# A hybrid decoder layer on one Trainium2 core: modulation sums, first loads and the whole hand-written order are rewritten

## Chip, core and metric

One core of one Trainium2 chip runs the whole layer as one program. The time is the device time of one execution in microseconds; lower is better. Engines: TensorE (PE, matrix products; its loads of the stationary operand are listed as PEld), VectorE (DVE), ScalarE (ACT), GpSimd (POOL), SyncE (SP, issues DMAs). ScalarE has a DMA queue as well, which is called the second queue here.

## The reference, cut to what matters

x is 256 x 1024, c is 1 x 1024, all in float32, one layer:

```python
mod = c @ w_ada + b_ada                                  # 1024 -> 3072
shift, scl, gate = split(mod, 3)
h = rms_norm(x, g_norm) * (1 + scl) + shift
proj = h @ w_in                                          # 1024 -> 5120
u_pool, z_pool, q, k, v, z_attn, m_pool, m_attn = split(proj)
y_pool = (multiscale_pool(u_pool) * silu(z_pool)) @ w_pool_up
y_attn = (attention(rope(q), rope(k), v) * silu(z_attn)) @ w_attn_up
merged = sigmoid(m_pool) * y_pool + sigmoid(m_attn) * y_attn
out = rms_norm(x + gate * (merged @ w_out), g_final)
```

With 256 positions and attention blocks of 256 there is one block, so the attention is plain causal attention of 8 heads of 64.

## The kernel before, in words

**Split products.** Each product with a weight runs as three products on rounded operands: a weight `raw` as loaded is rounded by ScalarE to `whi` (token `hi`, L223), VectorE forms the rest `wlo = raw - whi` (token `lo`, L227), and the activations are split the same way (hh and hl). The three are whi·hh, whi·hl and wlo·hh. So each unit of weights passes DMA, then ScalarE, then VectorE, then TensorE.

**Units.** The weights are cut into units. A0 to A7 are the rows k of w_in for q, k and v (768 KB each, one k block of 128 rows and 1536 columns). F1, F3, F5a, F5b, U, ZP, ZAa, ..., MA1b hold parts of the other columns of w_in, UP0 to UP3 the up projections, OUT0 to OUT3 w_out, G0 to G3 the part of w_ada for the gate, at most 1 MB each. A unit takes one of five `raw` buffers, and whi and wlo have three buffers each. `LOADS` is the order of the loads, all on SP's queue; `pump` (L199) is called when the last split of a unit is written and queues the next loads for which a buffer is free. Integers in `LOADS` are the parts of w_ada for shift and scale: 0, 1, 4, 5, 6 and 7 are one block of 128 outputs (1 MB), 2 covers blocks 2 and 3 (2 MB). 4 and 5 reuse the tile of 0 and 1, and 6 and 7 that of 2, so they wait for these. SP issues in order: a load that waits for its buffer holds up all behind it.

**The order.** `PROGRAM` is a list of tokens; a loop at the end of the kernel turns each into a call by the dictionary `table`, and each engine executes its own instructions in the order in which the tokens stand. Engines wait for one another by data and buffers alone. So the place of a token counts against those of the same engine.

**Start.** x is loaded in two halves of 128 rows. ScalarE squares (L412), GpSimd forms rstd, VectorE scales (xn, L418), TensorE transposes in blocks of 128 (`x`, L348), ScalarE copies the blocks from PSUM to xnT (`xc`, L351). `warm` is a transpose of the identity into a bank that is overwritten later; it gives nothing to the result (L309). The modulation of block k: either VectorE sums eight products with c over the tile (`mod_acc`, L263 and L265), or TensorE does it against c repeated in 32 columns (`mod_pe`, L291), or half each, and `mod_out` brings the sum to SBUF (L299, L302). It then stands spread over 128 partitions. `mod_fin` (L318) multiplies it by a column of ones, which sums over the partitions and gives one value per partition; `mod_add` adds the bias and multiplies the scale by the norm weight (L326, L327). Then `hh` (L358), `h` (L365) and `hl` (L368) make the split activations of block k.

**Projections.** `ap` is one of the three passes of a unit A for one of three column groups i and one of two row blocks t, 128x512 (L387); `a` is all three. The six results stay in six PSUM banks over all k. `f` is a job of an F unit, three 128x256 products for each of its k blocks (L372 to L374). `evac` brings q, k and v to SBUF, `rope` rotates, `tr` and `trc` transpose, `sc` are the scores; softmax, attention and the pooling follow.

**End.** `up` forms the up projections, `mg` to `mgl` the gated merge, `out:f:n` adds the part of feature block f to output bank n (banks 0 and 1: rows 0 to 127; 2, 3 and 4: rows 128 to 255, of 512, 256 and 256 columns). The gate is a row: `gate:0` to `gate:7` sum on VectorE, `gatef` (L668) sums over partitions, `gatec` copies it, writes it to DRAM and reads it back to all partitions as gg (L676, L677). `res` multiplies a bank by gg (L741), `resx` adds x, `sq` squares, `rstd` runs on GpSimd, `weigh`, `sact` and `sdve` scale, `store` writes out.

Of the kernel before, what the change touches and what calls it, by code (L numbers as in the profile page):

```python
# [78 lines left out]
ap:0:2:1:2 ap:1:1:0:0 ap:0:0:0:2 ap:1:0:0:0 hl:1 ap:1:0:0:1 hi:F1:0:512 ap:1:0:1:0 lo:F1:0:512 ap:1:1:1:1 f:F1:0
f:F1:1 ap:1:1:1:0 hi:F1:512:1024 lo:F1:512:1024 hi:A1:1024:1536 ap:1:2:1:0 f:F1:2 mod_acc:2:0:4 f:F1:3 hi:F1:1024:1536  # L80
lo:F1:1024:1536 ap:1:1:0:1 lo:A1:1024:1536 mod_pe:2:4:8 hi:F1:1536:2048 mod_out:2 ap:1:2:1:1 ap:1:2:0:2 ap:1:2:0:0
ap:0:1:1:1 fin:F1:0 fin:F1:1 hi:A2:512:1024 hi:A2:0:512 hi:A2:1024:1536 lo:A1:512:1024 mod_fin:2:0 mod_fin:2:1
mod_add:2:0 h:2 hh:2 ap:1:1:0:2 ap:1:2:0:1 f:F1:4 f:F1:5 mod_add:2:1 ap:1:0:1:1 ap:2:2:1:0 ap:2:1:0:0 h:3 ap:1:0:0:2
# [786 lines left out]
```

## Time and profile before

| | us |
|---|---|
| median of 3 runs (lowest to highest) | 204.57 (204.27 to 205.05) |
| the profiled execution | 204.59 |
| its span, first to last instruction | 202.8 |

| engine | busy, us | share of the span | instructions |
|---|---|---|---|
| TensorE products | 191.3 | 94% | 1412 |
| TensorE loads of operands | 172.3 | 85% | 1412 |
| VectorE | 153.6 | 76% | 278 |
| ScalarE | 111.4 | 55% | 195 |
| GpSimd | 6.5 | 3% | 19 |

The DMA engines moved 46.73 MB, 230 GB/s in the mean. The mean granted clock of TensorE was 0.994 of full speed. How to read it: the page is of one execution, and times count from its first instruction. Products are pipelined, and a busy TensorE need not be at its peak; the distance between the starts of neighbouring products says more. In the chain of waits each piece is the work that the next one waited for. "[0.32 <-DVE hh]" behind a row means that the engine was idle 0.32 us before it and what ended that.

### The profile page before, as it was taken

Reading aid. Unit: us, or ns where it says so; the run is one execution under the profiler, and the core shown is the slowest. Engines: PE = TensorE matmul, PEld = TensorE weight load, DVE = VectorE, ACT = ScalarE, POOL = GpSimd, SP = SyncE. Lnnn points to the kernel's source line nnn. Section 1 sums busy time; section 2 is a strip of 40 time slices with the busy share of each in tenths; the row PEclk is TensorE's granted clock in tenths of the full one; section 3 lists DMA queues with packets and bytes.
Section 4 is the critical chain, followed back from the end, with each engine's and each line's share of the span. In section 5 each row is a group of like instructions: output and inputs, shape, how many; then the busy total and the mean of one; then the engine's idle time right before and its main releaser. Section 6 shows DMA issues by size and latency. Waiting matters only on the chain.

```text
span 202.8 us, 3615 instructions
## 1 busy us (share of the span) xinstructions
PE 191.3 (94%) x1412; PEld 172.3 (85%) x1412; DVE 153.6 (76%) x278; ACT 111.4 (55%) x195; POOL 6.5 (3%) x19
## 2 busy tenths in 40 slices
...
GB/s 158 385 424 411 414 314 253 387 419 417 346 205 239 207 158 86 224 204 7 367 259 207 124 247 160 175 194 378 414 419 74 207 210 0 140 171 5 0 103 103
DMA packets 10921, 46.73 MB, mean 230 GB/s; under 512 B 1684, under 2 KB 2584, under 8 KB 8216
## 3 DMA queue, kind: packets, MB, share of 16 engines
...
q10 hardware_dynamic: 576, 0.41, 0.7%
q8 instruction: 11, 0.18, 0.3%
...
q0 software_dynamic: 32, 0.00, 0.0%
HBM read 45.44 MB, written 1.05 MB: 229 GB/s over the span
## 4 chain that ended last, share of the span: by engine, by line
PE 77%; DMA 13%; issue 3%; DVE 2%; ACT 1%; SPq 1%; POOL 1%; POOLq 0%; DVEq 0%; ACTq 0%
PE acc L372 15%; PE acc L373 14%; PE acc L374 14%; PE acc L387 12%; DMA ada<-in_ada_one_dram 10%; PE misc L372 4%; PE misc L373 4%; PE misc L374 4%; DMA x<-in_x_dram 3%; PE misc L291 2%; PE acc L472 1%; PE acc L541 1%; PE acc L594 1%; PE misc L318 1%; SPq L196 1%
## 5 line engine op out<-in xcount | busy, mean ns | idle before, releaser
L227 DVE TENSOR_TENSOR wlo<-raw,whi 128x1024 fp32r<-128x1024 f32 (+2 forms) x70 | 68.2, 1007 | 15.3 <-ACT whi L223 14.8
L223 ACT CAST whi<-raw 128x1024 fp32r<-128x1024 f32 (+2 forms) x70 | 57.9, 876 | 26.1 <-PE acc L387 7.7
L372 PE MATMUL acc<-hh,whi 128*128 128x256 f32 x168 | 47.9, 285 | 0.0
L373 PE MATMUL acc<-hh,wlo 128*128 128x256 f32 x168 | 46.9, 279 | 0.0
L374 PE MATMUL acc<-hl,whi 128*128 128x256 f32 x168 | 46.8, 279 | 0.0
L372 PEld LDWEIGHTS acc<-hh,whi 128*128 128x128 f32 x168 | 31.6, 188 | 0.6 <-DVE stat L491 0.3
L373 PEld LDWEIGHTS acc<-hh,wlo 128*128 128x128 f32 x168 | 31.6, 188 | 0.1
L374 PEld LDWEIGHTS acc<-hl,whi 128*128 128x128 f32 x168 | 31.6, 188 | 0.0
L387 PE MATMUL acc<-whi,hh 128*128 128x512 f32 x42 | 15.6, 406 | 0.4 <-DVE hh L358 0.3
L372 PE MATMUL misc<-hh,whi 128*128 128x256 f32 x56 | 15.7, 280 | 0.0
L373 PE MATMUL misc<-hh,wlo 128*128 128x256 f32 x56 | 15.6, 279 | 0.0
L374 PE MATMUL misc<-hl,whi 128*128 128x256 f32 x56 | 15.6, 279 | 0.0
L387 PE MATMUL acc<-whi,hl 128*128 128x512 f32 x42 | 15.4, 401 | 0.0
L387 PE MATMUL acc<-wlo,hh 128*128 128x512 f32 x42 | 14.9, 404 | 0.0
L373 PE MATMUL acc<-whi,mhl 128*128 128x512 f32 (+1 forms) x40 | 13.9, 348 | 0.0
L372 PE MATMUL acc<-whi,mhl 128*128 128x512 f32 (+1 forms) x40 | 13.9, 348 | 0.0
L374 PE MATMUL acc<-wlo,mhl 128*128 128x512 f32 (+1 forms) x40 | 13.9, 346 | 0.0
L373 PEld LDWEIGHTS misc<-hh,wlo 128*128 128x128 f32 x56 | 10.5, 188 | 0.4
L372 PEld LDWEIGHTS misc<-hh,whi 128*128 128x128 f32 x56 | 10.5, 188 | 0.4
L265 DVE SCALAR_TENSOR_TENSOR adacc<-ada,vT,adacc 128x256 f32<-128x256 f32 (+1 forms) x19 | 10.0, 527 | 0.7
L374 PEld LDWEIGHTS misc<-hl,whi 128*128 128x128 f32 x56 | 10.5, 188 | 0.0
L309 PE MATMUL acc<-ident 128*128 128x128 f32 x52 | 9.1, 336 | 1.4 <-POOL ident masks.py:199 1.4
...
## 6 DMA issues: line engine op xcount, KB each, us to landing
raw<-in_weights_dram SPq DMA_DIRECT2D x19, 1024.0 KB, 4.9
...
ada<-in_ada_one_dram SPq DMA_DIRECT2D x11, 512.0 KB, 8.9
ada<-in_ada_two_dram SPq DMA_DIRECT2D x4, 512.0 KB, 11.6
g<-in_weights_dram SPq DMA_DIRECT2D x2, 1024.0 KB, 8.5
...
x<-in_x_dram SPq DMA_DIRECT2D x2, 512.0 KB, 5.9
raw<-in_x_dram SPq DMA_DIRECT2D x1, 1024.0 KB, 5.1
```

The source lines that it names most:

```text
L196: nc.sync.dma_start(t[:, i:i + step], weights[:, OFFSET[u] + i:OFFSET[u] + i + step])
L223: nc.scalar.copy(halves[u][0][:, a:b], raws[u][:, a:b])
L227: nc.vector.tensor_tensor(lo[:, a:b], raws[u][:, a:b], hi[:, a:b].bitcast(F32), op=ALU.subtract)
L265: nc.vector.scalar_tensor_tensor(a, t[:, kt], cT[:, kt:kt + 1], a, op0=ALU.mult, op1=ALU.add)
L291: nc.tensor.matmul(peb[k][r0:r0 + 32, 0:2 * n * P], c_rep[:, kt], t[:, kt].rearrange("p s n -> p (s n)"), start=kt < 4 or k in sums, stop= ...
L309: nc.tensor.transpose(banks_qkv[0][1][:, 0:P], ident, ident)
L318: nc.tensor.matmul(r[:, s:s + 1], sums[k][:, s, i * P:(i + 1) * P], ones[:, 0:1], start=True, stop=True)
L372: nc.tensor.matmul(o, ah, bh, start=start, stop=False)
L373: nc.tensor.matmul(o, al, bh, start=False, stop=False)
L374: nc.tensor.matmul(o, ah, bl, start=False, stop=stop)
L387: nc.tensor.matmul(banks_qkv[i][t], act[:, k, t * P:(t + 1) * P], halves[f"A{k}"][w][:, i * 512:(i + 1) * 512], start=k == 0 and p == 0, s ...
L472: nc.tensor.matmul(bv[j][:, i], qkT[0][r, h // 2, t * P:(t + 1) * P], qkT[0][r, 4 + h // 2, 0:nkeys], start=True, stop=True)
```

## The change

It does the following:

- The vector of small parameters (vT: c, norm weight, biases) is loaded first on the second queue, ahead of a first piece of ada 0 that is now two k blocks instead of one; the rest of ada 0 comes in pieces of four and two k blocks.
- xnT takes the norm weight already when it is copied from PSUM, block by block: blocks 0 and 1 on ScalarE, 2 to 7 on VectorE. The modulation no longer multiplies by it.
- For all blocks but 0, the sum over partitions is made by transposing the sums on TensorE (`mod_tr`) and reducing along the free axis on VectorE (`mod_red`), in place of the products with ones; one small add then gives shift and scale together.
- The loads have another order.
- All of `PROGRAM` is new.

The code, with the order cut to the places named later:

```diff
 LOADS = """
-A0 1 A1 F1 2 A2 A3 F3 A4 4 5 F5a A5 F5b 6 7 A6 consts ZP A7 MP0b U MP1b ZAa ZAb MP0a MP1a G0 G1 MA0a MA0b MA1b
-MA1a UP1 UP0 OUT0 OUT1 UP3 UP2 gf OUT2 OUT3 xr
+A0 1 A1 F1 2 A2 A3 F3 4 A4 6 F5a 5 A5 7 A6 F5b U A7 ZAb MP0b ZP consts MP1a MP0a MA0a ZAa MA1b MP1b MA0b G0 UP1 MA1a
+UP3 G1 OUT0 UP0 UP2 OUT2 xr OUT1 OUT3 gf
 """.split()
 PROGRAM = """
-warm:30 x:0:1:0 x:1:1:0 x:2:2:0 x:4:2:0 x:6:2:0 warm:3 x:0:1:1 x:1:1:1 xc:0:1 x:2:2:1 xc:1:1 x:4:2:1 xc:2:2 x:6:2:1
-warm:2 mod_pe:0:0:4 xc:4:2 warm:5 mod_pe:0:4:8 mod_out:0 warm:6 mod_fin:0:0 mod_add:0:0 hi:A0:0:512 hh:0 warm:6 h:0
+warm:32 x:0:1:0 x:1:1:0 x:2:2:0 x:4:2:0 x:6:2:0 mod_pe:0:0:2 mod_pe:0:2:6 warm:3 x:0:1:1 xc:0:1:0 mod_pe:0:6:8
+mod_out:0 x:1:1:1 x:2:2:1 x:4:2:1 x:6:2:1 xc:1:1:0 mod_fin:0:0 xc:2:2:1 mod_add:0:0 hi:A0:0:512 hh:0 h:0 warm:8 hl:0
+xc:4:2:1 xc:6:2:1 hi:A0:512:1024 ap:0:0:1:0 ap:0:0:0:0 ap:0:0:0:1 ap:0:0:1:1 hi:A0:1024:1536 lo:A0:0:512 mod_pe:1:0:8
+mod_out:1 ap:0:1:0:0 ap:0:1:0:1 ap:0:2:0:0 ap:0:2:0:1 mod_tr:1 ap:0:1:1:0 ap:0:1:1:1 lo:A0:512:1024 ap:0:0:1:2
...
+hh:7 ap:6:0:0:0 h:7 ap:7:1:1:0 hl:7 ap:6:1:0:1 ap:7:1:0:0 ap:7:2:0:1 ap:7:1:1:1 ap:7:0:0:1 ap:7:2:0:0 lo:A7:0:768
+ap:5:2:0:2 ap:6:0:0:1 ap:5:2:1:0 ap:5:1:1:1 ap:7:0:0:0 lo:A7:768:1536 ap:7:1:0:1 ap:7:1:0:2 hi:ZP:0:1024 ap:6:0:1:0
+lo:ZP:0:1024 ap:6:2:1:2 ap:6:2:1:0 ap:7:2:1:1 ap:5:0:0:2 ap:7:2:1:0 hi:ZP:1024:2048 ap:7:2:1:2 ap:7:1:1:2 evac:1:1
+evac:1:0 ap:5:0:0:0 hi:U:0:1024 ap:5:0:0:1 ap:6:2:0:2 ap:7:0:0:2 evac:0:0 ap:7:0:1:1 ap:7:0:1:0 lo:ZP:1024:2048
+ap:6:0:1:2 ap:7:0:1:2 evac:0:1 hi:ZAb:1024:1536 f:ZP:0 f:ZP:1 lo:U:0:1024 f:U:2 evac:2:1 f:U:3 f:U:0 f:U:1 rope:1
+fin:ZP:0 rope:0 tr:1 fin:F5b:0 tr:3 hi:ZAb:0:1024 hi:MP0a:0:1024 hi:MP0a:1024:1536 fin:U:1 fin:U:0 tr:0 trc:0 trc:3
...
+mg:3 mgl:5 mga:3 mgh:3 gate:7 gatef mgl:3 mg:2 out:4:4 mg:7 mga:7 mga:2 hi:OUT1:1024:2048 mgh:2 hi:OUT1:0:1024
+lo:OUT1:1024:2048 out:3:2 out:3:0 out:3:1 mgh:7 mgl:2 lo:OUT1:0:1024 out:5:1 out:2:1 out:2:4 out:3:4 out:2:2 gatec
+mg:6 mga:6 hi:OUT3:0:1024 hi:OUT3:1024:2048 lo:OUT3:0:1024 lo:OUT3:1024:2048 out:3:3 mgh:6 mgl:6 out:2:0 out:6:0
+out:5:0 out:2:3 mgl:7 out:7:0 res:0 resx:0 out:6:1 out:7:1 res:1 resx:1 sq:0:0 sq:1:0 weigh:0 out:5:2 out:6:2 weigh:1
+out:4:2 out:7:2 res:2 resx:2 out:5:3 out:6:3 out:4:3 out:7:3 res:3 resx:3 sq:2:0 out:6:4 out:5:4 out:7:4 mean:0 res:4
+resx:4 sq:3:0 mean:1 rstd:0 sact:0 store:0:0 sq:4:1 rstd:1 sact:1 store:1:0 weigh:2 sact:2 sdve:4:0 store:4:1
+store:2:0 sdve:3:0 store:3:1
 """
     xs = work.tile([P, NT, D], F32, name="x", tag="qk", bufs=1)
+    nc.scalar.dma_start(vT, vecs)
...
-        for i in range(0, NK, step):
-            a = i
-            if k == i == 0:
-                nc.scalar.dma_start(t[:, 0:1], src[:, 0:1])
-                nc.scalar.dma_start(vT, vecs)
-                a = 1
-            nc.sync.dma_start(t[:, a:i + step], src[:, a:i + step])
+        ends = (2, 6, 8) if k == 0 else range(step, NK + 1, step)
+        for i, j in zip((0, *ends), ends):
+            queue = nc.scalar if k == i == 0 else nc.sync
+            queue.dma_start(t[:, i:j], src[:, i:j])
...
+    def mod_tr(k):
+        n = 1 if k in ONES else 2
+        sum_banks[k] = misc()
+        for i in range(n):
+            for s in range(2):
+                nc.tensor.transpose(sum_banks[k][:, (2 * i + s) * P:(2 * i + s + 1) * P],
+                                    sums[k][:, s, i * P:(i + 1) * P], ident)
+        used.add(k)
+        pump()
+
+    def mod_red(k):
+        n = 1 if k in ONES else 2
+        r = work.tile([P, 4], F32, name="modr")
+        nc.vector.tensor_reduce(r[:, 0:2 * n], sum_banks[k][:, 0:2 * n * P].rearrange("p (a b) -> p a b", b=P), axis=AX.X,
+                                op=ALU.add)
+        nc.vector.tensor_tensor(mods[:, k:k + n], r[:, 0:2 * n].rearrange("p (a b) -> p a b", b=2), bias[:, k:k + n],
+                                op=ALU.add)
+
     def mod_add(k, i):
-        r, ks = sum_banks[k][:, 2 * i:2 * i + 2], slice(k + i, k + i + 1)
-        nc.vector.tensor_scalar(scale[:, ks], r[:, 1:2], bs1[:, ks], gT[:, ks], op0=ALU.add, op1=ALU.mult)
-        nc.vector.tensor_tensor(shift[:, ks], r[:, 0:1], bT[:, ks], op=ALU.add)
+        nc.vector.tensor_tensor(mods[:, k + i], sum_banks[k][:, 2 * i:2 * i + 2], bias[:, k + i], op=ALU.add)
...
-    def x_copy(k, n):
-        nc.scalar.copy(xnT[:, k:k + n].rearrange("p a b -> p (a b)"), xbanks[k][:, 0:n * S])
+    def x_copy(k, n, dve):
+        for j in range(n):
+            src, g = xbanks[k][:, j * S:(j + 1) * S], gT[:, k + j:k + j + 1]
+            if dve:
+                nc.vector.tensor_scalar(xnT[:, k + j], src, g, None, op0=ALU.mult)
+            else:
+                nc.scalar.activation(xnT[:, k + j], src, AF.Copy, scale=g)
```

`bias` holds b_ada of shift and 1 + b_ada of scale side by side, made by two small VectorE instructions at the start, and `mods` shift and scale side by side; `hh` and `h` read them from there.

## Rows read from the trace of the kernel before

**Rows 1.** The page's table of engines: busy us (share of the span) xinstructions.

```profile
PE 191.3 (94%) x1412; PEld 172.3 (85%) x1412; DVE 153.6 (76%) x278; ACT 111.4 (55%) x195; POOL 6.5 (3%) x19
```

**Rows 2.** Stretches: us, busy of PE, PEld, DVE, ACT, POOL, granted clock, DMA share, GB/s.

```profile
0.00:30.00 30.00, 26.91 (x184) 21.12 (x185) 13.97 (x32) 15.60 (x30) 3.08 (x14) 1.00 0.91 352
30.00:40.00 10.00, 10.00 (x64) 8.91 (x63) 9.45 (x19) 5.59 (x9) 0.00 (x0) 1.00 0.89 315
100.00:120.00 20.00, 20.00 (x173) 20.00 (x172) 18.07 (x36) 15.39 (x21) 0.00 (x0) 1.00 0.60 211
```

**Rows 3.** Timeline, start: begin us, us, engine, line, operation [idle before <-releaser].

```profile
7.33 0.29 DVE L245 TENSOR_SCALAR c_rep<-vT 128x256 f32<-128x256 f32 x1 [7.33 <-DMA vT<-in_vecs_dram]
...
9.31 0.92 DVE L418 TENSOR_SCALAR xn<-x,rstd 128x512 f32<-128x512 f32 x2 [0.82 <-POOL rstd L334]
...
12.36 0.64 PE L291 MATMUL misc<-ada,c_rep 128*32 128x256 f32 x8
...
13.64 0.52 PE L318 MATMUL misc<-ones,adapart 128*128 128x1 f32 x4
...
14.64 0.41 DVE L358 TENSOR_SCALAR hh<-xnT,scale,shift 128x256 fp32r<-128x256 f32 x1
...
15.20 0.71 PE L387 MATMUL acc<-whi,hh 128*128 128x512 f32 x2 [0.32 <-DVE hh L358]
```

**Rows 4.** Chain of waits in order of time: begin us, us, what.

```profile
1.20 5.93 DMA x<-in_x_dram
...
19.43 0.34 PE misc L318 x4
...
68.22 9.33 PE acc L387 x40
...
85.91 0.87 PE misc L453 x8
```

**Rows 5.** Timeline, 17 to 50 us: SP's issues, hh, and TensorE's wait.

```profile
17.64 0.33 SPq L196 DMA_DIRECT2D raw<-in_weights_dram  x1
...
28.60 1.28 SPq L196 DMA_DIRECT2D raw<-in_weights_dram  x3
...
29.53 0.41 DVE L358 TENSOR_SCALAR hh<-xnT,scale,shift 128x256 fp32r<-128x256 f32 x1
...
49.72 1.07 PE L291 MATMUL misc<-ada,c_rep 128*32 128x256 f32 x16 [1.41 <-DMA ada<-in_ada_one_dram]
```

**Rows 6.** Groups by line and form: xcount | busy us, mean ns | idle before <-releasers.

```profile
L227 DVE TENSOR_TENSOR wlo<-raw,whi 128x1024 fp32r<-128x1024 f32 x39 | 46.6, 1221 | 10.6 <-ACT whi L223 10.6
...
L326 DVE TENSOR_SCALAR scale<-misc,bs,vT 128x1 f32<-128x1 f32 x8 | 2.2, 276 | 7.8 <-ACT whi L223 4.0 <-PE misc L318 3.8
...
L489 DVE TENSOR_TENSOR pr<-acc,mask 128x256 f32<-128x256 f32 x4 | 1.7, 418 | 0.0
...
L223 ACT CAST whi<-raw 128x1024 fp32r<-128x1024 f32 x39 | 39.5, 1049 | 12.5 <-PE acc L387 5.9 <-issue 3.6 <-PE acc L374 1.1
...
L365 ACT ACTIVATE h<-xnT,shift,scale 128x256 f32<-128x256 f32 x8 | 4.6, 597 | 9.4 <-DVE shift L327 9.4
...
L351 ACT COPY xnT<-misc 128x256 f32<-128x256 f32 x1 | 0.4, 373 | 1.9 <-PE misc L348 1.9
```

**Rows 7.** DMA issues: operand, queue, xcount, KB each, median us to landing.

```profile
raw<-in_weights_dram SPq DMA_DIRECT2D x19, 1024.0 KB, 4.9
...
gg<-gdram SPq DMA_DIRECT2D x1, 512.0 KB, 3.7
```

**Rows 8.** Timeline, end: gate row and last output banks.

```profile
174.02 0.64 PE L668 MATMUL misc<-gg,ones 128*32 128x256 f32 x8
...
178.86 0.33 SPq L677 DMA_DIRECT2D gg<-gdram  x1
...
188.22 0.69 DVE L741 TENSOR_TENSOR r<-acc,gg 128x512 f32<-128x512 f32 x1 [1.69 <-PE acc L374]
...
195.85 0.42 DVE L741 TENSOR_TENSOR r<-acc,gg 128x256 f32<-128x256 f32 x1 [0.18 <-PE acc L374]
```

More of the change, by code (lines that the diff above doesn't have):

```diff
@@ L79 @@
[L79 to L83, printed above, removed]
@@ L119 @@
-hi:UP2:0:1024 lo:UP2:0:1024 hi:UP2:1024:2048 lo:UP2:1024:2048 up:0:0 gate:6 up:1:1 mg:1 fin:MA1b:0 hi:OUT0:1024:2048
-hi:OUT0:0:1024 up:0:1 mg:0 up:4:0 up:4:1 up:5:0 gate:5 up:5:1 mga:1 lo:OUT0:1024:2048 lo:OUT0:0:1024 mga:0 mgh:0
-gate:7 up:2:0 mgl:0 up:2:1 fin:MA1a:0 mg:4 mga:4 up:3:0 up:3:1 fin:MA0b:0 mgh:1 mgl:1 out:0:3 hi:UP3:1024:2048 out:0:0
-out:1:3 hi:UP3:0:1024 lo:UP3:0:1024 out:0:1 out:1:1 hi:OUT1:1024:2048 hi:OUT1:0:1024 out:0:2 out:1:2 mg:3 mga:3 mgh:3
-mgh:4 mgl:4 out:0:4 out:1:4 mgl:3 lo:OUT1:1024:2048 out:3:4 out:3:3 out:1:0 out:3:1 mg:5 mga:5 gatef lo:OUT1:0:1024
@@ L124 @@
-gatec up:7:0 lo:UP3:1024:2048 up:7:1 mgh:5 hi:OUT2:1024:2048 hi:OUT2:0:1024 out:3:2 mg:2 mga:2 up:6:0 up:6:1
-lo:OUT2:0:1024 out:4:1 out:4:0 mgh:2 mgl:2 out:2:3 mg:7 out:3:0 mga:7 out:2:1 mgh:7 out:2:0 out:2:4 mgl:7 out:2:2
-lo:OUT2:1024:2048 hi:OUT3:0:1024 lo:OUT3:0:1024 hi:OUT3:1024:2048 mgl:5 out:5:0 mg:6 mga:6 mgh:6 lo:OUT3:1024:2048
-mgl:6 out:6:0 out:7:0 out:6:1 res:0 resx:0 out:5:1 out:7:1 res:1 resx:1 sq:0:0 weigh:0 sq:1:0 out:4:2 mean:0 rstd:0
-sact:0 out:5:2 out:6:2 out:7:2 store:0:0 res:2 weigh:1 sact:1 out:6:3 store:1:0 resx:2 sq:2:0 out:4:3 out:5:3 out:7:3
@@ new lines @@
+lo:MP0b:0:1024 hi:MP0b:1024:1536 pool:0 f:ZAa:1 fin:ZAa:0 lo:MP0b:1024:1536 f:MP0a:0 f:MP0a:1 scm:1:1:2 scm:1:5:2
+fin:ZAb:0 exp:0:0:4 hi:MP1a:0:1024 hi:MP1a:1024:2048 lo:MP1a:0:1024 lo:MP1a:1024:2048 exp:1:4:2 norm:1:4:2 f:MP0b:0
+f:MP0b:1 fin:MP0a:0 f:MP1a:0 f:MP1a:1 exp:1:1:2 norm:1:1:2 att:1 exp:1:5:2 hi:MP1b:0:1024 hi:MP1b:1024:2048
+lo:MP1b:1024:2048 lo:MP1b:0:1024 f:MP1b:0 fin:MP0b:0 sco:1:0:2 silu:2560:1 hi:MA0a:0:1024 f:MP1b:1 hi:MA0a:1024:2048
+scm:1:0:2 lo:MA0a:1024:2048 lo:MA0a:0:1024 f:MA0a:0 f:MA0a:1 exp:1:0:2 norm:1:0:2 silu:512:0 silum:512:0
```

90 lines of the change are left out of this document (43 added, 47 removed).

## The prediction

> **What bounds the kernel now.** I read the busy table first: TensorE is busy for 94% of the span, VectorE for 76%, ScalarE for 55% [rows 1]. A busy share hides where the limit changes, so next came the stretches [rows 2]. From 100 to 120 us TensorE is busy for all 20 us at granted clock 1.00, its 2.4 GHz level; from 30 to 40 us it is full as well, and VectorE beside it works 9.45 of 10. Whether full means packed is read from the chain of waits in order of time [rows 4]: 40 projection passes of 128x512 in a row take 9.33 us, 0.233 each, and long pieces like this one, on TensorE alone, fill it from 15.2 to 195.8 us, where the last product ends. So the time is: a start, 180.6 us of nearly gapless TensorE work, and a tail. An edit pays only if it starts that stream earlier, takes a hole or an instruction out of it, or shortens the tail; what it moves on other engines counts only where TensorE then waits.
>
> The start is read from the timeline [rows 3]. The second half of x lands at 7.1 us [rows 4]; square, rstd and the scaled xn follow (9.31) [rows 3], then its transposes, and only after these stand in TensorE's queue the modulation products of block 0 (those of its last four k blocks, eight instructions, at 12.36), the ScalarE copy, the ones-products (13.64), the modulation, hh (14.64) and the first pass (15.20). The two inputs of hh, x and modulation, are made one after the other. c_rep waited for vT until 7.33, on a queue where 128 KB of weights stood before it. The one large hole in the stream lies before 49.72: 1.41 us for an ada tile [rows 5]. Its load stood on SP behind A4, which waited for a buffer: SP issued nothing from 17.64 to 28.60.
>
> The profiled execution took 204.59 us, with 1.79 outside its span of 202.8; the median of the runs is 204.57, so I sum against the profiled one and carry the 1.79.
>
> **The start.** In the new order the products of six of the eight k blocks stand before the second-half transposes, those of the last two behind the first of these. x1 sets the chain: on the second queue now 274 KB run beside x instead of 146, which I price at 0.35 us (128 KB at the 352 GB/s that the first 30 us show [rows 2] is 0.37; bounds 0 and 0.6, should x meanwhile get less than half). So xn at 9.65, the first transpose at 10.2. Then ScalarE: the xc block with the norm weight as scale, not shown in the trace; it lies between the plain copy of the same size (0.37) and h, which has a scale and a bias (0.60) [rows 6]; I take 0.50, as it differs from h by the bias alone. It ends at 11.1, the copy of the sums at 11.5, the ones-products at 12.0, modulation and hh (0.41) at 12.75. Against 15.20 the first pass comes at **12.95** (warm:8 fills TensorE until then): 2.25 us gained. Bounds: 12.3, if the copy costs 0.37 and x is not delayed; 13.9, if x comes 0.6 late and each ScalarE step is as slow as h.
>
> The Trainium skill, "DMA: Bandwidth & Descriptors", section "Queues, rings and completion order", says that each DMA engine goes round robin between the queues that have work. That speaks against the larger piece on the second queue, since x is what the chain waits for. By it x would lose the time of the 128 KB, as taken above; the sum without it would be 0.35 lower. No row here shows the two queues with this load.
>
> Block copies 2 to 7 go to VectorE: six, from PSUM, near 0.42 (the 128x256 add from PSUM [rows 6]; 0.35 to 0.45 does not matter). Two stand before mod_add and end at 11.8, under the ones-products; four (1.7 us) stand after hl:0, and behind them waits lo:A0:0:512, ready near 15.9, wanted after eight passes, the products of block 1 and its transposes at 16.7. The cover is 0.8 us; without it this costs up to 1.7.
>
> **Transposed sums.** After the first pass seven ones-product calls go (0.34 each [rows 4]) and 14 transposes come (0.87 for eight, 0.11 each [rows 4]): TensorE wins 2.38 - 1.54 = **0.84 us**. VectorE reduces 128x256 from PSUM (not shown; by the same add 0.42, at least the 0.28 of the small op that it replaces [rows 6], at most twice 0.42) for that 0.28; the small add is there both times. Five blocks: +0.7 us, bounds 0 and 2.8, beside 153.6 us of work [rows 1]; it counts only where VectorE is late, below.
>
> **Load order and middle.** Up to F3 the loads are the same, so ada 2 and A2 come as before and hh:2 (29.53 [rows 5]) can't come earlier. Before the first pass of block 2 the new order has 36 passes and eight F1 jobs, the old had 32 and six: 4 x 0.233 + 2 x 0.70 = 2.3 us more. That fills just the 2.25 gained: TensorE reaches block 2 at about 30.3 in both. From there VectorE is nearly full (9.45 of 10 [rows 2]) with hl, four splits and eight ada sums before block 4. Laying its instructions end to end from hh:2 I get a:3:0:1 wanted at 32.5 and its split done at 33.0, and waits near hl:1 and mod_out:2 of some tenths. I take 0.6 us for these, bounds 0 and 2.25 (all of the gain).
>
> ada 4 is now loaded before A4, 6 before F5a; A1's last split stands 3.9 us of TensorE work earlier, and it is that split which frees A4's buffer. The first 30 us move 10.5 MB [rows 2], which is all up to F3; at 2.5 to 3 us per MB behind it ada 6 and 5 land by 38 and 43, wanted at 44: the hole of 1.41 goes, and the next late load is not in this stretch.
>
> The later one is ZP. It is issued after ZAb and MP0b, when lo:A6:768:1536 is done, by my count at 64.8; a 1 MB load lands 4.9 us after issue [rows 7], so at 70. Its first cast is wanted at 69.0, and cast (1.05) and split (1.22) [rows 6] end at 72.3; f:ZP:0 is wanted at 72.7. ScalarE's evictions queue behind that cast, then rope on VectorE; rope ends at 79.0 where tr:1 is wanted at 78.3. I take 0.7, bounds 0 and what rival D gives. For all other waits of the new order, which I can't follow one by one, 0.3.
>
> **Tail.** Both orders end with the same chain: last product, two VectorE ops, square, rstd, scale, stores. It was 7.0 us from 195.8 to the end of the span [rows 8]. New: the scalings and stores of rows 0 to 127 come after the last products and rstd:0 stands before rstd:1 on GpSimd; ScalarE does its two scalings while VectorE makes the last sums, and the last stores go out on both queues, as before. I take +0.3 (0 to 1.0).
>
> The gate row is tighter: from the end of gatef (174.66) to the landing of gg (178.86 + 3.7) it took 7.9 us [rows 7, 8]; the old order had 13.3 us of products there before bank 0 was done, the new has 8.7 (ten 512-wide jobs of three products, 0.70, and five halves). At nothing, if ScalarE has OUT1's casts behind it when gatef ends.
>
> **Sum.** By the same count (passes 0.233, jobs by their products, transposes 0.11) the old stream is 173.2 us and the trace 180.6: 1.4 is the hole, 6.0 small waits and slots a little longer than the count, which I carry over. New: 12.95 + 172.4 + 6.0 = 191.35; plus 0.6 + 0.7 + 0.3 of new waits = 192.95; plus the tail 7.3 and 1.79: **202.0 us**, 2.6 below before.
>
> **Rivals.**
> A, no new wait: the same sum without the 1.6 and the 0.3, 200.1 us. For it: VectorE idles 10.6 us in front of its wide splits [rows 6], so later on TensorE alone is full. Against it: 30 to 40 us, where VectorE has half a microsecond to spare.
> B, VectorE takes the start back: block 2 and 3 wait for its splits, the lead of 2.25 is lost there and only the hole and the 0.84 remain: 203.7. For it rows 2; against it the 2.3 us of extra work that the order puts before block 2.
> C, the gate row is late: OUT1's two casts, two mgh copies and only then gatec stand on ScalarE after gatef; if all run behind it, 2.9 us pass, and 7.9 + 2.9 is 2.1 more than 8.7. VectorE's ops from res:0 on (eight at 0.69, two at 0.42 [rows 8]: 6.4 us) fill the 6.65 us of products left, so the tail moves nearly whole: 204.1. Against it: these casts need only a buffer that comes free 3 us before.
> D, slower: ZP late. The queue SP is in order, ZP behind two loads that wait for splits, and behind ZP's cast stand four PSUM evictions without which the next banks can't be opened. Each microsecond that ZP lands after 70.4 is one of TensorE; from a landing at 74.0 the kernel is slower than before, at 75.5 it takes 207. For it: VectorE would have to be 4 to 5 us late with lo:A6, as it may be after the full stretch. Against it: the 10.6 us for which it idles before such splits.
>
> **How the numbers follow.** Forecast 0.45 (200.9 to 203.2), A 0.22, B 0.11, C 0.09, D 0.13. Half a percent, about what a measurement can tell, is 1.0 us: faster means below 203.5, which A, the forecast and a third of B give, 0.69; B's rest and most of C are within it, 0.18; D gives slower, 0.13. The range runs from 199.8, just below A, to 205.2, over C and the first of D.
>
> **What would show it.** The first pass at 12.95 (12.3 to 13.9); the first block-2 pass near 30.3; no wait for ada from 40 to 60; a wait under 1 us at the transposes near 78; the last product at 192 to 194; 7 to 7.6 us behind it. Wrong: TensorE's idle time before 40 us over 2 us after its first pass, a cast of ZP waiting for its load past 72, or the first residual waiting for gg.

## The result, and the profile after

The changed kernel took **199.65 us** (median of 4 runs, 199.43 to 199.80) against 204.57 before (median of 4 runs in the record, 204.27 to 205.05; the section ahead counts 3): ratio 0.9756 (95% interval 0.9735 to 0.9778), 4.9 us less. The forecast was 202.0 with a range of 199.8 to 205.2: the sign is right, the size is missed just below the range. The profiled execution took 199.80, with a span of 198.0. In the changed kernel the lines from L358 to the end of the projections stand 23 further down (L387 is now L410, L372 to L374 are L395 to L397), the split is L221 and L225 and the residual L764.

The page's table of engines of the changed kernel, against [rows 1]:

```profile
PE 188.5 (95%) x1389; PEld 168.8 (85%) x1389; DVE 156.7 (79%) x282; ACT 107.5 (54%) x190; POOL 6.5 (3%) x19
```

Its stretches, with the columns of [rows 2]:

```profile
0.00:30.00 30.00, 27.56 (x186) 21.59 (x186) 18.03 (x39) 15.33 (x28) 3.08 (x14) 1.00 0.95 365
30.00:40.00 10.00, 10.00 (x61) 8.70 (x60) 9.64 (x18) 5.24 (x8) 0.00 (x0) 1.00 1.03 405
40.00:50.00 10.00, 10.00 (x70) 7.93 (x69) 9.07 (x21) 4.55 (x9) 0.26 (x1) 1.00 0.90 364
...
13.00:190.00 177.00, 177.00 (x1310) 159.19 (x1309) 149.58 (x261) 98.84 (x174) 1.94 (x3) 1.00 0.64 236
```

The last row is the main one: from 13 to 190 us TensorE has no idle time at all that the trace shows, the stretch from 40 to 50 with its old hole [rows 5] included. VectorE is as full from 30 to 40 as before and a little fuller (9.64 against 9.45 [rows 2]), and still no product waits for it. The loads of operands, which run beside the products, do wait for VectorE, six times between 14 and 67 us, by 0.16 to 0.28 each, one of them at a:3 (0.17 at 33.86); the product behind starts at most 0.11 late.

The timeline of the changed kernel at the places that the prediction names (begin us, us, engine, line, operation, [idle before <-releaser]), against [rows 3, 5, 8]:

```profile
4.28 0.29 DVE L243 TENSOR_SCALAR c_rep<-vT 128x256 f32<-128x256 f32 x1 [4.28 <-DMA vT<-in_vecs_dram]
...
7.84 1.06 ACT L435 ACTIVATE junk<-x 128x1024 f32<-128x1024 f32 x1 [2.59 <-DMA x<-in_x_dram]
...
9.62 0.64 PE L291 MATMUL misc<-ada,c_rep 128*32 128x256 f32 x8 [0.64 <-DMA ada<-in_ada_one_dram]
...
9.98 0.92 DVE L441 TENSOR_SCALAR xn<-x,rstd 128x512 f32<-128x512 f32 x2 [2.85 <-POOL rstd L351]
...
12.16 0.50 PE L318 MATMUL misc<-ones,adapart 128*128 128x1 f32 x4
...
12.96 0.41 DVE L381 TENSOR_SCALAR hh<-xnT,mods 128x256 fp32r<-128x256 f32 x1
...
13.52 0.71 PE L410 MATMUL acc<-whi,hh 128*128 128x512 f32 x2
...
29.26 0.42 DVE L381 TENSOR_SCALAR hh<-xnT,mods 128x256 fp32r<-128x256 f32 x1
...
33.27 0.40 PE L397 MATMUL acc<-wlo,hh 128*128 128x512 f32 x1
...
61.76 0.33 SPq L194 DMA_DIRECT2D raw<-in_weights_dram  x1
...
70.17 2.00 ACT L221 CAST whi<-raw 128x1024 fp32r<-128x1024 f32 x2 [4.08 <-PE acc L410]
...
77.91 0.43 DVE L464 TENSOR_TENSOR pqk<-ra,rb 128x256 f32<-128x256 f32 x1
...
78.61 0.60 PE L476 MATMUL acc<-ident,pqk 128*128 128x128 f32 x4
...
178.07 0.33 SPq L700 DMA_DIRECT2D gg<-gdram  x1
...
184.41 0.69 DVE L764 TENSOR_TENSOR r<-acc,gg 128x512 f32<-128x512 f32 x1 [3.48 <-PE acc L397]
...
191.01 0.42 DVE L764 TENSOR_TENSOR r<-acc,gg 128x256 f32<-128x256 f32 x1
```

So the first pass comes 1.68 us earlier than in [rows 3] (13.52), the last residual 4.84 earlier than in [rows 8] (191.01), and the 3.16 between them were won inside the stream. There I took the distance from the start of each product to the start of the next in both traces and summed it by kind. The products with ones and the transposes that replace most of them went from 2.63 us to 1.06 (-1.57, for 28 products and 14 transposes; block 0's call, which stands ahead of the first pass, is in neither); the 128x512 passes became 1.54 shorter, which is the hole; every other kind is equal within 0.2. From the last residual to the end of the span it is 7.0 us, as before.

The chain of waits of the changed kernel in order of time (begin us, us, what): a call with ones, four transposes in its place for blocks 2 and 3, and a long run of passes, against [rows 4].

```profile
12.32 0.34 PE misc L318 x4
...
27.80 0.50 PE misc L330 x4
...
64.19 8.97 PE acc L410 x38
```

The four transposes serve two blocks, which took two calls of 0.34 before, and the passes stand where they stood (0.236 each). The groups by line and form of the changed kernel (xcount | busy us, mean ns | idle before) give what VectorE pays:

```profile
L225 DVE TENSOR_TENSOR wlo<-raw,whi 128x1024 fp32r<-128x1024 f32 x39 | 46.6, 1221 | 7.3 <-ACT whi L221 7.3
...
L372 DVE TENSOR_SCALAR xnT<-acc,vT 128x256 f32<-128x256 f32 x6 | 2.5, 476 | 1.0 <-PE acc L365 1.0
...
L338 DVE TENSOR_REDUCE modr<-misc 128x2 f32<-128x256 f32 x5 | 2.1, 420 | 2.5 <-PE misc L330 2.5
```

### The profile page after: what moved, and what is told of

Its sections match the earlier page's. It is cut to its first block, busy times and chain, and to the rows that moved or that the text cites. A ratio compares the mean times of both kernels' runs of the same rounds, so it can differ in the third digit from the quotient of the medians.

```text
span 198.0 us, 3564 instructions
## 1 busy us (share of the span) xinstructions
PE 188.5 (95%) x1389; PEld 168.8 (85%) x1389; DVE 156.7 (79%) x282; ACT 107.5 (54%) x190; POOL 6.5 (3%) x19
## 3 DMA queue, kind: packets, MB, share of 16 engines
HBM read 45.44 MB, written 1.05 MB: 235 GB/s over the span
## 4 chain that ended last, share of the span: by engine, by line
PE 88%; DMA 4%; DVE 3%; issue 1%; POOLq 0%; SPq 0%; ACT 0%; POOL 0%; DVEq 0%
PE acc L410 15%; PE acc L395 15%; PE acc L396 15%; PE acc L397 15%; PE misc L396 5%; PE misc L395 5%; PE misc L397 5%; DMA ada<-in_ada_one_dram 4%; PE misc L291 2%; PE acc L495 1%; DVE r L769 1%; PE acc L564 1%; DVE r L764 1%; PE acc L617 1%; PE misc L330 1%
## 5 line engine op out<-in xcount | busy, mean ns | idle before, releaser
L221 ACT CAST whi<-raw 128x1024 fp32r<-128x1024 f32 (+2 forms) x70 | 58.2, 875 | 31.2 <-PE misc L397 8.1
L225 DVE TENSOR_TENSOR wlo<-raw,whi 128x1024 fp32r<-128x1024 f32 (+2 forms) x70 | 68.0, 1007 | 8.9 <-ACT whi L221 8.8
L395 PE MATMUL acc<-hh,whi 128*128 128x256 f32 x168 | 47.4, 282 | 0.0
L397 PE MATMUL acc<-hl,whi 128*128 128x256 f32 x168 | 46.9, 279 | 0.0
L395 PEld LDWEIGHTS acc<-hh,whi 128*128 128x128 f32 x168 | 31.6, 188 | 0.4 <-DVE stat L514 0.3
L397 PEld LDWEIGHTS acc<-hl,whi 128*128 128x128 f32 x168 | 31.6, 188 | 0.0
L410 PE MATMUL acc<-whi,hh 128*128 128x512 f32 x42 | 15.9, 408 | 0.0
L395 PE MATMUL misc<-hh,whi 128*128 128x256 f32 x56 | 15.7, 281 | 0.0
L397 PE MATMUL misc<-hl,whi 128*128 128x256 f32 x56 | 15.6, 279 | 0.0
L410 PE MATMUL acc<-whi,hl 128*128 128x512 f32 x42 | 15.2, 403 | 0.0
L410 PE MATMUL acc<-wlo,hh 128*128 128x512 f32 x42 | 15.0, 404 | 0.0
L395 PE MATMUL acc<-whi,mhl 128*128 128x512 f32 (+1 forms) x40 | 14.0, 350 | 0.0
L397 PE MATMUL acc<-wlo,mhl 128*128 128x512 f32 (+1 forms) x40 | 13.9, 346 | 0.0
L395 PEld LDWEIGHTS misc<-hh,whi 128*128 128x128 f32 x56 | 10.5, 188 | 0.3
L397 PEld LDWEIGHTS misc<-hl,whi 128*128 128x128 f32 x56 | 10.5, 188 | 0.0
L410 PEld LDWEIGHTS acc<-wlo,hh 128*128 128x128 f32 x42 | 7.8, 188 | 2.8 <-issue 1.2
```

The costliest lines, as they stand in the source:

```text
L221: nc.scalar.copy(halves[u][0][:, a:b], raws[u][:, a:b])
L225: nc.vector.tensor_tensor(lo[:, a:b], raws[u][:, a:b], hi[:, a:b].bitcast(F32), op=ALU.subtract)
L395: nc.tensor.matmul(o, ah, bh, start=start, stop=False)
L397: nc.tensor.matmul(o, ah, bl, start=False, stop=stop)
L410: nc.tensor.matmul(banks_qkv[i][t], act[:, k, t * P:(t + 1) * P], halves[f"A{k}"][w][:, i * 512:(i + 1) * 512], start=k == 0 and p == 0, s ...
```

## The experiments

**Part by part out of the changed kernel.** The first four ran on one chip, where the kernel before took 204.44.

`e1_ones`: the sums as products with ones again, in the new order, for block 1 and alike for 2 and 4 to 7.

```diff
-mod_tr:1 ... mod_red:1
+mod_fin:1:0 ... mod_add:1:0
```

> The changed kernel with one part undone: the sums of blocks 1, 2 and 4 to 7 go back to products with a column of ones and the small add that block 0 uses; order, loads and all else stay. Theory S (the stream of products has no waits left, so each product taken out or put in counts in full): in the two traces seven such calls took 2.63 us of TensorE's slots and the transposes in their place 1.06, so 199.7 + 1.6 = 201.3 us. Theory V (what counts is VectorE's chain from sum to hh, and TensorE's slots are covered): the chain gets shorter by 0.1 to 0.2 us a block, no change within 0.4 us, 199.3 to 200.1.

Measured: 200.70 (200.56 to 200.78), ratio 0.9816 (0.9794 to 0.9839), so 1.05 us above the changed kernel: the gain of the transposes is real and reaches the end, a little less than the 1.57 of its slots. The two traces agree: this execution starts its first pass 0.50 earlier (13.02) and ends its products 0.75 later, so its stream is 1.25 longer.

`e2_loads`: the head of the loads in the old order, all else new.

```diff
-... F3 4 A4 6 F5a 5 A5 7 A6 F5b U ...
+... F3 A4 4 5 F5a A5 F5b 6 7 A6 U ...
```

> The changed kernel with the old order of loads between F3 and A6 (A4 4 5 F5a A5 F5b 6 7 A6); the rest of the loads and the order of work stay as changed. Theory L (the hole of 1.4 us before the products of block 6 was made by the place of ada 6 in the queue): ada 6 comes after ada 5, F5a, A5 and F5b again, 3.5 MB later than now, near 46 to 47 us where TensorE wants it at 44 to 45: the hole is back with 1.5 to 3 us, 201.2 to 202.7 us. Theory A (the hole came from the late split of A1, which held up the buffer of A4; the new order splits A1 earlier and this alone ends it): 199.7 within 0.4.

Measured: 204.56 (203.33 to 205.66), ratio 0.9999 (0.9971 to 1.0027). The whole gain is gone, more than either theory said; on the cause theory L is right and theory A is not (SP issues A4 from 22.17 on here, where [rows 5] have 28.60, so A1's early split does free the buffer, and the hole is back all the same). The timeline of this run and its stretches (columns of [rows 2]; the execution in the profile took 205.66):

```profile
45.68 0.35 DVE L263 TENSOR_SCALAR adacc<-ada,vT 128x256 f32<-128x256 f32 x1 [3.30 <-DMA ada<-in_ada_one_dram]
...
47.51 0.42 DVE L391 TENSOR_TENSOR hl<-h,hh 128x256 fp32r<-128x256 f32 x1
...
47.98 0.79 PE L410 MATMUL acc<-whi,hl 128*128 128x512 f32 x1 [3.15 <-DVE hl L391]
```

```profile
46.00:48.00 2.00, 0.02 (x1) 0.02 (x1) 1.89 (x6) 0.00 (x0) 0.00 (x0) 0.80 1.04 422
48.00:54.00 6.00, 6.00 (x25) 3.47 (x26) 4.23 (x8) 0.00 (x0) 0.26 (x1) 0.50 0.11 45
54.00:56.00 2.00, 2.00 (x12) 1.61 (x11) 1.39 (x5) 0.83 (x2) 0.00 (x0) 1.00 0.00 0
```

VectorE waits 3.30 us for the ada tile of block 6, and hl of block 4, which has nothing to do with it, stands behind that sum in VectorE's order; TensorE waits for hl. Then it runs at its lower level, 1.2 GHz: the granted clock is 0.50 from 48 to 54. The wait of 3.15 and the half of six slow microseconds are 6.2, and this execution is 5.9 above the changed one. The kernel before had waited 1.41 us [rows 5] at clock 1.00.

`e3_start`: the first loads as before (one k block of ada 0 on the second queue, then vT).

```diff
-    nc.scalar.dma_start(vT, vecs)
-        ends = (2, 6, 8) if k == 0 else range(step, NK + 1, step)
+                nc.scalar.dma_start(t[:, 0:1], src[:, 0:1])
+                nc.scalar.dma_start(vT, vecs)
```

> The changed kernel with the first loads as before: on the second queue one k block of ada 0 (128 KB) and then the small vectors, the rest of ada 0 behind x in pieces of three and four k blocks. Theory X (the 256 KB beside x on the second queue delay x's second half by 0.7 us, and x sets the chain to the first product): x's second half lands near 6.8 instead of 7.5, the first product of block 0 at 12.9 instead of 13.5; 199.0 us if the whole lead passes to the end, 199.3 to 199.4 if only the 0.35 us that the split of A3 had to spare. Theory W (the small vectors first are what makes the start earlier): c_rep waits until 7.3 on VectorE with xn behind it, the start is no better than now, 199.7 to 200.3.

Measured: 199.58 (199.38 to 199.61), ratio 0.976 (0.9738 to 0.9782): no difference. c_rep comes at 7.03 there and the first pass still at 13.26. The new first loads as a whole bring nothing. The trace shows two effects that cancel: with the smaller piece beside it x's second half is squared at 6.85, 0.99 earlier than in the changed kernel, but the late vectors now set the chain (it leads from the landing of vT to c_rep, bias and xn).

`e4_xfirst`: only vT on the second queue, all of ada 0 on SP behind x.

```diff
-            queue = nc.scalar if k == i == 0 else nc.sync
+            queue = nc.sync
```

> The changed kernel with the small vectors alone on the second queue and all pieces of ada 0 on SP behind x. Theory X: nothing but 18 KB runs beside x, its second half lands at 6.3 to 6.6, the first product comes at 12.3 to 12.7; the time is 198.7 us if this lead of 1 us passes to the end, 199.3 if it is cut by VectorE's splits after block 2, which were 0.35 us ahead of TensorE. Theory Y (the products of block 0 wait for ada instead, as ada's pieces now come behind x): no gain, 199.7 within 0.3.

Measured: 199.22 (198.92 to 199.43), ratio 0.9743 (0.972 to 0.9767). Its timeline:

```profile
5.85 1.06 ACT L435 ACTIVATE junk<-x 128x1024 f32<-128x1024 f32 x1 [0.26 <-DMA x<-in_x_dram]
...
9.01 0.64 PE L291 MATMUL misc<-ada,c_rep 128*32 128x256 f32 x8 [0.23 <-DMA ada<-in_ada_one_dram]
...
12.89 0.70 PE L410 MATMUL acc<-whi,hh 128*128 128x512 f32 x2
```

The chain of waits of this run has, up to the second of these rows:

```profile
2.12 6.84 DMA ada<-in_ada_one_dram
```

The square of x's second half begins 2.0 us earlier than in the changed kernel, the first pass only 0.63, because x no longer sets the chain: the eight products at 9.01 wait for block 0's weights, and the first pass follows 3.88 behind them. In the six runs with the changed kernel's first loads (the changed kernel itself, e1, e2, e6, e7, e12b) the first pass comes 5.68 or 5.69 behind x's second square, whenever that is; here it is 7.04. The 0.63 reach the end whole.

**Parts put into the kernel before.** `e5_tr_old`: only the transposes and the reduce, for block 1 and alike for 2 and 4 to 7.

```diff
-mod_fin:1:0 mod_add:1:0
+mod_tr:1 mod_red:1
```

> The kernel before, with its own loads, order and start, where the two sums of block 1 on (the ones-products on TensorE and the small additions behind them) are replaced by the transposes into one PSUM tile and one reduce on VectorE with the old additions behind it. Theory S (the transposes are shorter wherever they stand, and TensorE is the bound): the inverse of the run that put the products back, -1.05 to -1.6, so 203.0 to 203.5. Rival V (VectorE is full between 30 and 50 in the old order, and the reduce of 0.42 us per block comes back in the split that TensorE waits for): 203.8 to 204.8.

Measured: 204.71 (204.18 to 206.51), ratio 1.0032 (1.0005 to 1.0059): nothing won. Timeline of this run, and one stretch:

```profile
28.95 0.69 DVE L338 TENSOR_REDUCE modr<-misc 128x4 f32<-128x512 f32 x1 [0.25 <-PE misc L330]
...
30.19 0.41 DVE L379 TENSOR_SCALAR hh<-xnT,scale,shift 128x256 fp32r<-128x256 f32 x1
...
50.11 1.07 PE L291 MATMUL misc<-ada,c_rep 128*32 128x256 f32 x16 [1.91 <-DMA ada<-in_ada_one_dram]
```

```profile
48.00:50.00 2.00, 0.20 (x1) 0.00 (x0) 1.21 (x3) 0.67 (x1) 0.00 (x0) 1.00 1.05 421
```

hh:2 comes at 30.19, 0.66 later than in [rows 5], since the reduce and four small operations stand in front of it (the changed kernel has one small one, and hh at 29.26). Where the gain goes is read from the starts of the same products in both traces. Up to 20 us this run wins 0.23 and loses 0.45 by 22; the sums of blocks 2 and 3 win 0.38, and 0.32 are lost between 31 and 33. At these places TensorE's loads of operands wait for VectorE, as they do not in the kernel before:

```profile
20.94 0.19 PEld L408 LDWEIGHTS acc<-whi,hh 128*128 128x128 f32 x1 [0.38 <-DVE hh L379]
...
32.45 0.19 PEld L394 LDWEIGHTS misc<-hh,wlo 128*128 128x128 f32 x1 [0.38 <-DVE wlo L227]
```

That is rival V. The hole then grows from 1.41 to 1.91, 0.1 of it because TensorE arrives earlier and 0.39 because the load lands later; at the end the run is 0.06 behind.

`e9_loads_old`: only the head of the loads.

```diff
-... F3 A4 4 5 F5a A5 F5b 6 7 A6 consts ...
+... F3 4 A4 6 F5a 5 A5 7 A6 F5b consts ...
```

> The kernel before with one thing of the change: the order of the head of the list of loads (4 before A4, 6 before F5a, 5 before A5, 7 before A6). Everything else, the order of the work among it, is the old one. Theory L (the wait of 1.41 us before 49.72 was for the modulation block that this order loads earlier): 203.0 to 203.3, with no wait for a load between 40 and 60. Rival O (the old order of work then waits for A4 or F5a, which now come later): 204.4 to 205.5.

Measured: 203.02 (202.85 to 203.05), ratio 0.9934 (0.9911 to 0.9956). In its timeline the row that answers to 49.72 in [rows 5] has no wait:

```profile
48.12 1.07 PE L291 MATMUL misc<-ada,c_rep 128*32 128x256 f32 x16
```

So the hole is worth 1.35 us by itself, with the old order of work around it.

`e10_tr_loads`: e5 and e9 together, so that no hole can take what the transposes win.

> The kernel before with two things of the change: the head of the list of loads in the new order, and the transposes with one reduce for the sums of block 1 on. With the loads alone it took 203.02 and waited for no load. Theory S (the transposes brought nothing in the old order because the wait for the load behind them took the gain; that wait is gone here): 201.4 to 202.0. Rival V (in the old order TensorE also waits for VectorE's splits between 20 and 35, and the reduce makes these late): 202.7 to 203.3, with no gain by 33 us from the start.

Measured: 202.65 (202.53 to 203.34), ratio 0.9888 (0.984 to 0.9937). That is 0.4 below e9 by the medians, which ran on different chips, and 0.9 by the ratios, whose intervals overlap: how much is won is not settled, where it is won is. By the starts of the same products in the traces of e9 and e10, blocks 1 to 3 bring nothing by 33 us (0.11 behind e9 at 15 us, 0.29 behind at 33), which is rival V's sign. The loads of operands wait for hh at 21.00 and for a split at 32.50, as in e5. The sums of blocks 4 to 7 then win 0.64, to 0.35 ahead at 60. After 80 us this execution, the slowest of its six, loses 0.7 to other waits.

`e12_start_old`: e9 with the start's tokens in the new order, every operation and first load old.

```diff
-... x:6:2:0 warm:3 x:0:1:1 x:1:1:1 xc:0:1 ... x:6:2:1 warm:2 mod_pe:0:0:4 xc:4:2 warm:5 mod_pe:0:4:8 mod_out:0 ...
+... x:6:2:0 mod_pe:0:0:4 warm:3 x:0:1:1 xc:0:1 mod_pe:0:4:8 mod_out:0 x:1:1:1 x:2:2:1 x:4:2:1 x:6:2:1 xc:1:1 ...
```

> The kernel before with the new head of the list of loads, and the tokens of its start in the new order: the sums of block 0 on TensorE before and between the transposes of x's second half, not behind them. Operations, the first loads and the rest of the order are the old ones; with the loads alone it took 203.02, with its first pass at 15.09. Theory O (the order of the start alone makes the new start; first pass 13.0 to 13.5, and TensorE keeps it to the end): 201.0 to 201.6. Rival V (first pass as early, but the splits of the old order, late on VectorE or waiting for loads, take it back by 35 us): 202.4 to 203.1. Rival P (the start needs the vectors first, or the norm weight taken into the copy from PSUM): first pass 14.5 or later, 202.4 to 203.0.

Measured: 201.69 (201.39 to 203.18), ratio 0.9851 (0.9802 to 0.99), 1.3 below e9 by the medians, which ran on different chips. Its timeline:

```profile
13.27 0.71 PE L387 MATMUL acc<-whi,hh 128*128 128x512 f32 x2
...
14.90 0.50 PE L387 MATMUL acc<-whi,hh 128*128 128x512 f32 x1 [0.51 <-ACT whi L223]
```

The order alone brings the first pass to 13.27, with vT late and the norm weight where it was. Of the 1.8 us it keeps 1.2 to the end of the trace: at 14.90 TensorE waits 0.51 us for a cast that stands behind the block copies on ScalarE.

**Spare time.** `e6_zp_late`: ZP one load later.

```diff
-... ZAb MP0b ZP consts MP1a MP0a ...
+... ZAb MP0b consts MP1a ZP MP0a ...
```

> The changed kernel with the 1-MB load of ZP issued one load later (behind the consts and MP1a, in front of MP0a). In the changed kernel it landed at 69.5 at the latest and its cast at 70.17 waited for a PSUM buffer, not for it; here it would land near 72. Theory D, as the prediction priced it (each us past 70.4 costs one us of TensorE): 201.2 to 202.2. Rival, covered (the first product that needs ZP started 0.6 us after the last split, and other products are queued in front): 199.5 to 200.2.

Measured: 203.74 (201.95 to 206.24), ratio 0.995 (0.9923 to 0.9976), 4.1 us worse than the changed kernel. Its timeline and stretches:

```profile
73.01 1.99 ACT L221 CAST whi<-raw 128x1024 fp32r<-128x1024 f32 x2 [7.03 <-DMA raw<-in_weights_dram]
...
75.53 0.58 PE L395 MATMUL acc<-hh,whi 128*128 128x256 f32 x1 [2.48 <-ACT pqk L454]
...
78.88 0.28 PE L396 MATMUL acc<-hh,wlo 128*128 128x256 f32 x1
```

```profile
74.00:76.00 2.00, 0.47 (x2) 0.47 (x3) 1.92 (x2) 2.00 (x5) 0.00 (x0) 0.79 0.00 0
76.00:78.00 2.00, 2.00 (x11) 2.00 (x11) 1.50 (x2) 2.00 (x4) 0.00 (x0) 0.50 0.40 57
78.00:80.00 2.00, 2.00 (x17) 2.00 (x16) 1.33 (x5) 2.00 (x4) 0.00 (x0) 0.85 0.91 353
```

The cast now waits for the load, TensorE for a bank that ScalarE evicts behind that cast: rival D of the prediction, place and mechanism. (The expectation calls the buffer that this cast waits for in the changed kernel a PSUM buffer; the cast writes `whi`, and it waits for a pass that still reads one of its three.) To the 2.48 us of waiting comes the clock: until 78.6 a product takes 0.215 us instead of 0.117, for 14 of them 1.4 us more. 2.48 + 1.4 is 3.9 of the 4.1.

`e7_dve`: one addition of 128x512 on VectorE ahead of the split that a:3:0:1 takes; its result is used nowhere.

```diff
-hh:3 hl:3 ap:2:2:0:2 lo:A3:0:768 a:3:0:1
+hh:3 hl:3 dly ap:2:2:0:2 lo:A3:0:768 a:3:0:1
```

> The changed kernel with one additional addition of 128x512 (about 0.69 us) on VectorE ahead of the split of A3's low part, where the profile shows 0.35 us between the split's end and the product that takes it. Nothing else is changed; its result is used nowhere. Theory tight (no spare but these 0.35 us): 199.9 to 200.1, and a wait of 0.3 to 0.4 us for VectorE near 33. Rival ample (the wait is absorbed by products that can run first): 199.5 to 199.8 with no wait.

Measured: 200.09 (199.74 to 200.20), 0.44 above. Its timeline:

```profile
31.79 0.68 DVE L812 TENSOR_TENSOR dly<-part 128x512 f32<-128x512 f32 x1
...
33.40 0.49 PE L397 MATMUL acc<-wlo,hh 128*128 128x512 f32 x1 [0.16 <-DVE wlo L225]
```

In this trace TensorE falls 0.59 behind the changed kernel between 31 and 36 us and is 0.39 behind it at the end, where the 0.68 us less the spare 0.35 make 0.33. So the prediction's place was right, and the spare in the changed kernel is a third of a microsecond at most.

**More of the start.** `e11_start2`: e4, and all of block 0's sums before the transposes of x's second half.

```diff
-mod_pe:0:2:6 warm:3 x:0:1:1 xc:0:1:0 mod_pe:0:6:8 mod_out:0 x:1:1:1 x:2:2:1 ... xc:1:1:0 mod_fin:0:0 xc:2:2:1 mod_add:0:0 ...
+mod_pe:0:2:6 mod_pe:0:6:8 mod_out:0 x:0:1:1 x:1:1:1 x:2:2:1 xc:0:1:0 mod_fin:0:0 ... mod_add:0:0 ... xc:1:1:0 warm:4 hl:0 xc:2:2:1
```

> The changed kernel with two edits: block 0's modulation weights wholly on SP's queue behind x (that alone took 199.22, first pass 12.89), and in the start the last part of block 0's sums ahead of the transposes of x's second half, with the copies of the other blocks behind the first hh. Theory E (TensorE works without a gap from the first pass on, so what the start gives is the whole gain): first pass 12.1 to 12.4, 198.4 to 198.8. Rival W (the modulation weights or A0 land no earlier, and the first pass waits for them): first pass 12.8 to 13.0, 199.1 to 199.4. Rival B (the copies of the other blocks come too late for their passes): 199.3 to 200.0.

Measured: 199.65 (199.13 to 199.95), ratio 0.9736 (0.9692 to 0.9781): no gain. Its timeline:

```profile
12.61 0.71 PE L410 MATMUL acc<-whi,hh 128*128 128x512 f32 x2
...
13.02 2.44 DVE L372 TENSOR_SCALAR xnT<-acc,vT 128x256 f32<-128x256 f32 x6
...
21.51 0.28 PE L395 MATMUL misc<-hh,whi 128*128 128x256 f32 x1
```

The first pass is 0.28 earlier than in e4, but all six block copies now follow on VectorE, the splits are 0.5 later, and TensorE reaches this job, the first of F1, 0.49 later than in e4 (21.02). That is rival B in small.

`e12b_after_again`, `e13_xfirst_again` (e4 once more) and `e14_xc2_act` (e11 with two of these copies on ScalarE) ran on one chip.

> The changed kernel itself, beside the two below and on their chip, so that they are compared with it directly. 199.4 to 199.9, first pass 13.0 to 13.6.

> The changed kernel with block 0's modulation weights wholly on SP's queue behind x, once more and beside the changed kernel. Theory X (the 256 KB of these weights on the second queue delay x's second half, and what the start loses reaches the end): 0.3 to 0.6 below the changed kernel, x's second square 1 to 2 us earlier. Rival, none (the first comparison was the spread between chips): within 0.15 of it.

> The kernel with the earlier start that gained nothing (e11, 199.65, first pass 12.61 but first pass of block 2 at 21.51), with one edit: the copies of block 2 and 3 of x go from VectorE to ScalarE, behind the casts of A0, so VectorE has 0.8 us less in front of the splits. Theory B (VectorE's splits took that start back): first pass of block 2 at 20.6 to 20.9, 198.7 to 199.1. Rival A (TensorE lost it to something else, such as the load of block 1's sums): 199.4 to 199.8.

Measured: 199.53 (199.48 to 199.82), 199.31 (199.10 to 200.15) and 199.24 (199.01 to 201.25); ratios 0.9758 (0.9737 to 0.978), 0.9754 (0.9728 to 0.978) and 0.9746 (0.9719 to 0.9773). The medians of e4 are below those of the changed kernel each time, by 0.2 to 0.4, but the intervals overlap: no version is shown to beat it. The profiled execution of e13 took 200.15 and shows one reason why they scatter; its timeline:

```profile
9.04 0.62 PE L291 MATMUL misc<-ada,c_rep 128*32 128x256 f32 x4 [0.85 <-DMA ada<-in_ada_one_dram]
...
10.30 0.64 PE L291 MATMUL misc<-ada,c_rep 128*32 128x256 f32 x8 [0.63 <-DMA ada<-in_ada_one_dram]
...
14.18 0.71 PE L410 MATMUL acc<-whi,hh 128*128 128x512 f32 x2
```

The same kernel had its first pass at 12.89 in e4; here the second of these loads came 1.3 us later, and the first pass with it. The profile of e14 is of its slowest execution (201.25, first pass 13.26). It reached the job of 21.51 in e11 (which its expectation calls the first pass of block 2) at 21.84, 8.58 behind its first pass, against 8.90 in e11 and 8.13 in e4: the two copies give back 0.3 of what e11 lost there. Then TensorE waited 0.34 for a split on VectorE, so nothing is shown to be won.

## Why the prediction was right or wrong

What bounds the kernel was right: all 4.84 us lie in the start and in the stream of TensorE, and the tail is unchanged. The last product was forecast at 192.95 and came at 191.0. By its terms:

- **New waits, 0.6 + 0.7 + 0.3: none came. This is the step that failed**, and the time is that of rival A (200.1) less half a microsecond. At a:3:0:1 I let the job wait for its split from its first product on (32.5 against 33.0). The split was done at 32.9, as counted; but the job began at 32.80, and of its three products only the third takes wlo, at 33.27. e7 shows that the place is as tight as I said (0.35 us) and on the right side of it. The 0.7 of ZP was a wait at tr:1 for rope (79.0 against 78.3). Up to the split of ZP the times came out, in part by luck: VectorE had lo:A6 done at 61.7 and the load was issued at 61.76, 3 us earlier than I counted, but behind two others it took 7.2 us to land (68.98), not 4.9; and its cast at 70.17 waited for a `whi` buffer, not for the load. Its first split ended at 72.5 (counted 72.3), 0.5 before f:ZP:0 at 73.00. What I had wrong is the stretch behind it: from there rope took 5.9 us, not 6.7, and ended at 78.34, and tr:1 began at 78.61 without a wait. e6 shows that one load of delay would have made it the worst term of all.
- **Transposed sums, 0.84: 1.57 in slots, 1.05 in time (e1).** I took the transposes at 0.11 from the run of eight in [rows 4]; among passes one took 0.076 from start to start, and a product with ones 0.09, thus 0.376 a call instead of 0.34. The VectorE side was right (0.42 for the reduce), and so was that it counts only where VectorE is late: in the old order, with more small operations behind the reduce, the gain of blocks 1 to 3 is gone by 33 us (e5, e10).
- **The start, 2.25: 1.68**, between 2.2 and 1.6 by execution (first pass 13.02 in e1, 13.36 in e12b, 13.60 in e6, 13.52 here), inside its bounds. x's second half was priced 0.35 late and came 0.68 late (square at 7.84 against 7.16), and x does set the chain, though only just: block 0's weights, for which TensorE waited until 9.62, would alone have given nearly the same first pass (9.62 + 3.88, as in e4). ScalarE's scaled copy took 0.47 (0.50). The Trainium skill, "DMA: Bandwidth & Descriptors", section "Queues, rings and completion order", has each engine go round robin between queues with work. The traces agree in sign: 128 KB more there cost x 0.2 to 1.1 us, by execution. What won the start was the order of tokens alone (e12), not the new first loads (e3).
- **The hole of 1.41 goes: right**, 1.54 in slots, 1.35 alone (e9). Ada 6 and 5 landed at 38.9 and 43.3 (counted 38 and 43). Of the two reasons that the prediction gives for the hole, the place of ada 6 in the queue is the cause; the buffer that A4 waited for is not (e2, and e9, where ada 6 still stands behind A4).
- **First pass of block 2 at 30.3**: it came at 30.94, behind hh:2 at 29.26 (counted with 29.53), so the work put before block 2 did fill the time won. Rival B did not happen here; e11 shows it in a start where VectorE is 0.5 us later.
- **Tail +0.3: 0.05.** The gate row (rival C) was on time: gdram to gg took 1.8 us from issue to issue, gg was issued at 178.07, and with the 3.7 of [rows 7] it stood 2.6 us before 184.41; the last of OUT1's casts, ahead of gatec on ScalarE, began at 174.62, before gatef's products.

With the measured terms the sum closes: 202.04 less 1.6 (waits), 0.73 (sums), 0.13 (hole) and 0.25 (tail), plus 0.57 (start), is 199.9, against 199.80 in the profiled execution. That the sums and the start nearly cancel is luck.

Put together: loads -1.35 (e9), the start's order -1.3 (e12), the sums -0.4 (e10) make 3.1 of the 4.9 in the old order of work (up to 4.0 by the ratios, as e10 and e12 ran on another chip than e9). The rest is what the new order lets through, of the sums above all, which bring 1.05 there (e1); no run puts all three parts into the old order. The parts are not additive: without the loads the new order gains nothing (e2).
